# Hybrid SSD and pooling decoder step on one core: part-array stretches gathered, step sizes stored by group, and half products summed in PSUM

## The chip, the cores and the metric

The kernel runs on one core of a Trainium2 chip. The metric is the device time of one execution in microseconds (us): the median of three runs. Engines are named as in the profile: PE is TensorE's matmul, PEld its weight load, DVE is VectorE, ACT ScalarE, POOL GpSimd, SP SyncE, which issues most DMAs.

## The reference

One inference step of a trunk of two layers, an SSD (Mamba-2) layer and a causal pooling layer, each with adaLN modulation, RMSNorm, a gate and a residual, for a prompt of 1024 tokens and 8 samples of 8 new tokens, which the kernel lays side by side as 1088 columns. D_MODEL is 1024, D_INNER 2048; the scan has 8 groups of 4 heads (64 rows each), a state of 128 and chunks of 128 tokens, so 8 chunks in the prompt.

```python
zxbcdt = h @ w_in                                   # z, x, B, C, dt
xs, Bm, Cm = split(silu(conv4(xbc)))
dt = softplus(dt_raw + dt_bias); A = -exp(a_log)
acum = cumsum(dt * A, in the chunk)                 # cumulated decays
CB = einsum('bctgn,bcsgn->bctsg', C, B)
y_intra = (CB * exp(acum_t - acum_s) * mask) @ (x * dt)
chunk_states = einsum(B, exp(acum_end - acum), x * dt)
h_{c+1} = exp(acum_end) * h_c + chunk_states        # scan over chunks
y_inter = einsum(C, exp(acum), h_c)
out = rmsnorm_per_group((y_intra + y_inter + d_skip * x) * silu(z)) @ w_out
# pooling layer: uz = h @ w_in; windowed means of u; group matmul; * silu(z); @ w_out
```

## The kernel before, in words

**Products in three matmuls.** Every large product is made in fp32r from a high and a low half of both factors: three matmuls (hi*hi, hi*lo, lo*hi) into one PSUM bank (mm1, L179 to L184). ACT makes the high half, DVE or POOL the low one (split_half, L168 to L177).

**Front, about 100 to 360 us.** Twelve pairs of row blocks of the first projection (table FRONT, front_pairs L1412) and fourteen of the pooling layer's (fast_pairs L1036, about 1050 to 1340 us) go through fast_pair (L986): for the outputs u and z over two token halves of 544 columns, seven half products B11, B21, T2, T3, T1, T4, B22 in place of eight (Strassen's scheme in Winograd's form, with weight sums from w_sums L935 on POOL). A half product (product, L966) is 24 matmuls of 272 columns (L980 to L982) into two PSUM banks, about 3.0 us. DVE adds the results (add, L991) in SBUF; ACT makes one copy per pair (L1006). Between the pairs of kind b or x stands the causal convolution of the pair before (conv_tile L336): a chain of four steps per tile on DVE (L349) and then one Silu per tile on ACT (L352).

**Scan, about 364 to 930 us.** ssd_layer (L1458) drives scan_group (L504) for eight groups, and between its steps a second stream of full-array matmuls, the "fill" (beside: projections of later groups, then the output product). The table FILL (L51) says how many pieces of fill follow each step of a group. In a group, front(c) of a chunk makes B^T C and three transposes (L545, L549), the decays M on ACT (L556, L557) from acb, the cumulated decays of the group's 4 heads broadcast to 128 partitions by a DMA (load_ac L524), the scaled x, and Bt, B's transpose (L566). For two chunks at a time, states (L583) makes two S products (L588) and two updates of the state h: a POOL multiply (L596) and a DVE add (L597; for chunk 0 a copy, L593). Then rows (L601) makes y: matmuls M by x (L609) and h by C (L613), with 128x64 tiles, two of them side by side in the array. Part of the array is also used by the samples' transposes (L437), by Z (L628), the samples' y (L641, L644), adaLN's am (L253) and the sums of squares ms (L708). The program's scheduler orders each engine's instructions by priority; waits are by semaphores.

**Step sizes.** The cumulated decays ac are stored by one DMA as 128 partitions x 320; load_ac reads four rows of 512 B for each of 128 partitions.

## Time and profile before

| | |
|---|---|
| median of 3 runs | 1631.19 us (1631.13 to 1631.39) |
| profiled execution, its own time | 1633.98 us |
| span of the profiled execution, first to last instruction | 1632.2 us |
| mean granted TensorE clock | 0.994 |
| PE busy | 1601.1 us (98%), 12061 records |
| PEld busy | 1524.7 us (93%) |
| DVE, ACT, POOL busy | 1290.3 (79%), 816.7 (50%), 495.2 us (30%) |
| DMA | 275.60 MB, mean 169 GB/s |

PE's busy time is modelled, since matmuls overlap in the array: a row's duration is longer than the step to the next row. What a matmul costs is therefore read in the timeline as the distance from its start to the start of the next one. A timeline row "x4" holds four records in a run; a plain fp32 matmul leaves two records, one per pass, an fp32r matmul and a transpose leave one.

### The profile page before, as it was taken

How to read it: one execution, taken by the hardware profiler on the slowest of the kernel's cores; microseconds unless marked ns; L12 is line 12 of the kernel's file. 1: busy time of each engine (PE TensorE's matmuls, PEld its weight loads, DVE VectorE, ACT ScalarE, POOL GpSimd, SP SyncE). 2: the span in 40 equal slices, each digit the busy share in tenths (PEclk: the TensorE clock that was granted, in tenths of full speed). 3: DMA queues.
4: the chain of work that ended last, by engine and by line, in shares of the span. 5: the costliest groups of instructions: out<-in, count | busy, mean ns of one | idle time of the engine just before them, and what ended most of it. 6: DMA issues, size and time to landing. Idle time of an engine off the chain costs nothing.

```text
span 1632.2 us, 30956 instructions
## 1 busy us (share of the span) xinstructions
PE 1601.1 (98%) x12061; PEld 1524.7 (93%) x12061; DVE 1290.3 (79%) x2140; ACT 816.7 (50%) x1565; POOL 495.2 (30%) x527
## 2 busy tenths in 40 slices
PE   8999999999999999999999999999999999999997
PEld 6899999998899888988998899999999999999997
DVE  6875779777788888789887867988889867577876
ACT  6653334456776767575645536632322333333364
POOL 0233556511221202121212222366667640000241
PEclk9999999999999999999999999999999999999999
DMA  9422232264555554668898533043333369565783
GB/s 346 163 98 84 93 109 71 105 203 133 183 162 167 165 186 135 217 232 299 276 332 284 201 137 111 29 142 112 102 112 99 129 213 367 166 170 173 167 164 119
DMA packets 122306, 275.60 MB, mean 169 GB/s; under 512 B 18192, under 2 KB 59312, under 8 KB 122160
## 3 DMA queue, kind: packets, MB, share of 16 engines
q1 hardware_dynamic: 118128, 260.91, 46.8%
q0 software_dynamic: 4032, 12.72, 4.5%
q8 instruction: 95, 1.56, 0.4%
q14 instruction: 51, 0.42, 0.1%
HBM read 201.12 MB, written 70.23 MB: 166 GB/s over the span
## 4 chain that ended last, share of the span: by engine, by line
PE 82%; DVE 7%; DMA 5%; issue 3%; ACT 2%; POOL 1%; SPq 0%; DVEq 0%; ACTq 0%; POOLq 0%
PE st L982 11%; PE st L980 11%; PE st L981 11%; PE mm L182 10%; PE mm L184 10%; PE mm L183 10%; DMA acb<-acd 2%; PE op L1197 2%; PE op L1198 2%; PE op L1196 2%; PE y L609 2%; PE S L588 2%; PE y L613 2%; PE am L253 1%; PE tr L549 1%
## 5 line engine op out<-in xcount | busy, mean ns | idle before, releaser
L982 PE MATMUL st<-hh,w 128*128 128x272 f32 x832 | 240.8, 289 | 2.3 <-DVE w L176 2.3
L980 PE MATMUL st<-hh,w 128*128 128x272 f32 x832 | 240.2, 289 | 0.0
L981 PE MATMUL st<-hl,w 128*128 128x272 f32 x832 | 239.7, 288 | 0.0
L982 PE MATMUL st<-t,w 128*128 128x272 f32 x624 | 179.6, 288 | 0.0
L980 PE MATMUL st<-t,w 128*128 128x272 f32 x624 | 179.6, 288 | 0.0
L981 PE MATMUL st<-t,w 128*128 128x272 f32 x624 | 179.2, 287 | 0.0
L182 PE MATMUL mm<-hh,wh 128*128 128x364 f32 (+1 forms) x528 | 178.4, 338 | 0.1
L184 PE MATMUL mm<-hh,wl 128*128 128x364 f32 (+1 forms) x528 | 174.6, 331 | 0.0
L183 PE MATMUL mm<-hl,wh 128*128 128x364 f32 (+1 forms) x528 | 173.7, 329 | 0.0
L174 ACT ACTIVATE w<-wr 128x512 fp32r<-128x512 f32 x104 | 65.6, 631 | 190.4 <-PE st L982 156.8
L982 PEld LDWEIGHTS st<-hh,w 128*128 128x128 f32 x832 | 156.4, 188 | 3.4 <-DVE w L176 3.4
L980 PEld LDWEIGHTS st<-hh,w 128*128 128x128 f32 x832 | 156.7, 188 | 0.3 <-issue 0.3
L981 PEld LDWEIGHTS st<-hl,w 128*128 128x128 f32 x832 | 156.8, 188 | 0.0
L596 POOL TENSOR_TENSOR hd<-h,cd 128x256 f32<-128x256 f32 x56 | 47.1, 842 | 353.6 <-DVE h L597 195.4
L182 PE MATMUL mm<-gh,wh 128*128 128x364 f32 (+1 forms) x384 | 130.2, 340 | 2.1 <-ACT raw L419 2.1
L1197 PE MATMUL op<-b,w 128*128 128x272 f32 x448 | 129.0, 288 | 1.3 <-DVE b L1126 1.3
L1198 PE MATMUL op<-b,w 128*128 128x272 f32 x448 | 129.0, 288 | 0.7 <-DVE w L1170 0.7
L1196 PE MATMUL op<-b,w 128*128 128x272 f32 x448 | 129.6, 289 | 0.0
L184 PE MATMUL mm<-gh,wl 128*128 128x364 f32 (+1 forms) x384 | 127.1, 331 | 0.0
L183 PE MATMUL mm<-gl,wh 128*128 128x364 f32 (+1 forms) x384 | 126.7, 330 | 0.1
L980 PEld LDWEIGHTS st<-t,w 128*128 128x128 f32 x624 | 117.7, 189 | 0.0
L982 PEld LDWEIGHTS st<-t,w 128*128 128x128 f32 x624 | 117.3, 188 | 0.0
(293 smaller groups left out, 4613.7 us busy)
## 6 DMA issues: line engine op xcount, KB each, us to landing
wr<-win SPq DMA_DIRECT2D x48, 512.0 KB, 3.7
acb<-acd SPq DMA_DIRECT2D x64, 256.0 KB, 3.9
wr<-pin SPq DMA_DIRECT2D x32, 512.0 KB, 3.6
wr<-pout SPq DMA_DIRECT2D x28, 512.0 KB, 3.9
x<-x1d SPq DMA_DIRECT2D x24, 544.0 KB, 6.3
x1d<-x SPq DMA_DIRECT2D x22, 544.0 KB, 5.4
wr<-pout POOLq DMA_DIRECT2D x20, 512.0 KB, 5.5
x<-xT SPq DMA_DIRECT2D x16, 544.0 KB, 6.0
```

The lines of the kernel that those rows point to most:

```text
L174: self.nc.scalar.activation(hi, src, AF.Copy)
L182: nc.tensor.matmul(ps[:, :n], hi[:, k, :], ah[:, a:a + n], start=first, stop=False)
L183: nc.tensor.matmul(ps[:, :n], hi[:, k, :], al[:, a:a + n], start=False, stop=False)
L184: nc.tensor.matmul(ps[:, :n], lo[:, k, :], ah[:, a:a + n], start=False, stop=last)
L588: nc.tensor.matmul(S[:, 256 * i:256 * i + 256], Bt, xde.rearrange("p r q -> p (r q)"), start=True, stop=True)
L596: nc.gpsimd.tensor_tensor(out=hd, in0=h[-1], in1=cd.unsqueeze(2).to_broadcast([P, 4, 64]), op=ALU.mult)
L980: nc.tensor.matmul(ps[c][:, :QUART], hi[:, k], xh[:, t], start=(k == 0), stop=False)
L981: nc.tensor.matmul(ps[c][:, :QUART], hi[:, k], xl[:, t], start=False, stop=False)
L982: nc.tensor.matmul(ps[c][:, :QUART], lo[:, k], xh[:, t], start=False, stop=(k == 3))
L1196: nc.tensor.matmul(ps[:, :QUART], hi[:, k], xh, start=k == 0, stop=False)
L1197: nc.tensor.matmul(ps[:, :QUART], hi[:, k], xl, start=False, stop=False)
L1198: nc.tensor.matmul(ps[:, :QUART], lo[:, k], xh, start=False, stop=k == 7)
```

## The change

It has three parts.

**Part-array stretches gathered.** rows becomes visit: the matmuls of y for two chunks stand in one stretch of high priority, and the first of them waits for the second update of the state (`behind`), though their data need only the first. What else uses part of the array is placed right behind that stretch: adaLN's am behind the visits of chunks 0, 2 and 6 (ADA) and no longer among the projections, the samples' transposes and Z behind the one of chunk 4, the samples' y behind the one of chunk 6, ms of a group behind the first visit of the next one, and now in the PSUM bank S. FILL puts three pieces of fill ahead of a group's first step in groups 1 to 4.

On PE, in group 1, the first visit stood in two pieces with a matmul of the fill (mm) between them, and an S product in the first piece (y: output rows, M and xd: decays and scaled x, h: state, ea: scaled C):

```order
L609 MATMUL y_5143<-M_4979,xd_4988 64x128 x2
L609 MATMUL y_5144<-M_4979,xd_4988 64x128
L588 MATMUL S_5109<-xd_5076,Bt_5078 128x256
L609 MATMUL y_5144<-M_4979,xd_4988 64x128
L609 MATMUL y_5143<-M_5067,xd_5076 64x128 x2
L609 MATMUL y_5144<-M_5067,xd_5076 64x128 x2
L183 MATMUL mm_5159<-hl_668,wh_4835 128x360
L613 MATMUL y_5143<-ea_5060,h_5112 64x128 x2
L613 MATMUL y_5144<-ea_5060,h_5112 64x128 x2
L184 MATMUL mm_5159<-hh_667,wl_4836 128x360
```

In the changed kernel the same visit is one piece, followed by ms of group 0 and am:

```order
L185 MATMUL mm_5292<-hl_455,wh_4867 128x360
L622 MATMUL y_5062<-M_4990,xd_4999 64x128 x2
L622 MATMUL y_5063<-M_4990,xd_4999 64x128 x2
L622 MATMUL y_5062<-M_5012,xd_5021 64x128 x2
L629 MATMUL y_5062<-ea_5005,h_5031 64x128 x2
L622 MATMUL y_5063<-M_5012,xd_5021 64x128 x2
L629 MATMUL y_5063<-ea_5005,h_5031 64x128 x2
L752 MATMUL ms_5076<-z_4644,ones 32x272 x4
L256 MATMUL am_5081<-wr_4744,scp 32x256 x4
L256 MATMUL am_5081<-wr_4863,scp 32x256 x4
L555 MATMUL tr_5098<-xbc_4436,xbc_4179 128x128
```

So S and the fill no longer stand between the part-array matmuls.

At the second visit of group 1, PE had the matmuls that need no new state right behind S and the transposes, and 17 matmuls of fill (from the last row on) before those that need the first update:

```order
L588 MATMUL S_5263<-xd_5215,Bt_5217 128x256
L545 MATMUL tr_5278<-xbc_4520,xbc_4302 128x128
L549 MATMUL tr_5278<-kc,xbc_4796 128x128
L549 MATMUL tr_5278<-kc,xbc_4952 128x128
L549 MATMUL tr_5278<-kc,xbc_4302 128x128
L609 MATMUL y_5299<-M_5127,xd_5136 64x128 x2
L613 MATMUL y_5299<-ea_5120,h_5114 64x128 x2
L609 MATMUL y_5300<-M_5127,xd_5136 64x128 x2
L613 MATMUL y_5300<-ea_5120,h_5114 64x128 x2
L609 MATMUL y_5299<-M_5206,xd_5215 64x128 x2
L609 MATMUL y_5300<-M_5206,xd_5215 64x128 x2
L182 MATMUL mm_5319<-hh_393,wh_4997 128x364
```

Now there are four transposes and six matmuls of fill between the last S and the visit, whose first row waits for the second update:

```order
L596 MATMUL S_5164<-xd_5112,Bt_5114 128x256
L555 MATMUL tr_5183<-xbc_4436,xbc_4179 128x128
L557 MATMUL tr_5183<-kc,xbc_4675 128x128
L557 MATMUL tr_5183<-kc,xbc_4848 128x128
L557 MATMUL tr_5183<-kc,xbc_4179 128x128
L185 MATMUL mm_5292<-hl_617,wh_4867 128x360
L186 MATMUL mm_5292<-hh_616,wl_4868 128x360
L184 MATMUL mm_5292<-hh_668,wh_4867 128x360
L185 MATMUL mm_5292<-hl_669,wh_4867 128x360
L186 MATMUL mm_5292<-hh_668,wl_4868 128x360
L184 MATMUL mm_5292<-hh_707,wh_4867 128x360
L622 MATMUL y_5236<-M_5046,xd_5055 64x128 x2
```

The visit moved behind the fill, and all of it stands behind the wait.

**Step sizes by group.** They are stored as [chunk, head, token], by four DMAs and one for the samples, and load_ac reads one row of 2 KB for each partition.

**Half products in PSUM.** The order is B11, B21, T2, T1, T3, T4, B22. The banks X sum B11, T2, T3 and T4 one after the other, the banks Y sum T1 and B22. ACT keeps copies of X after B11, T2 and T3 (keep), so that the sums that end elsewhere can be formed by DVE; z's first half goes from X through ACT straight to its place, with its Silu.

On ACT, in a pair that follows one of kind b or x, before: the copy of the first product (u<-st), weight splits (w), the convolution's two Silus (xbc), a gate's Silu (z):

```order
L1006 ACTIVATE u_2345<-st_2350 128x272
L1006 ACTIVATE u_2345<-st_2351 128x272
L174 ACTIVATE w_2379<-sw_2216 128x512
L174 ACTIVATE w_2411<-wr_2181 128x512
L352 ACTIVATE xbc_2316<-xbc_2316 128x1088
L352 ACTIVATE xbc_2329<-xbc_2329 128x1088
L862 ACTIVATE z_2343<-z_2343 128x544
```

And now (u_2051 is the first copy, u_2052 the one after T2, then u_2051 again after T3):

```order
L1052 ACTIVATE u_2051<-st_2053 128x272
L1052 ACTIVATE u_2051<-st_2054 128x272
L176 ACTIVATE w_2088<-wr_1894 128x512
L176 ACTIVATE w_2117<-wr_1894 128x512
L359 ACTIVATE xbc_2019<-xbc_2019 128x1088
L359 ACTIVATE xbc_2032<-xbc_2032 128x1088
L1052 ACTIVATE u_2052<-st_2053 128x272
L1052 ACTIVATE u_2052<-st_2054 128x272
L176 ACTIVATE w_2150<-sw_1925 128x512
L176 ACTIVATE w_2182<-wr_1923 128x512
L1052 ACTIVATE u_2051<-st_2053 128x272
L1052 ACTIVATE u_2051<-st_2054 128x272
```

The copy after T2, on which T3's matmuls into the same banks wait, stands behind the two Silus.

The diff, cut to its core:

```diff
-FILL = (((1,) * 10 + (2,),) * 4 + ((1,) * 9 + (4, 5),) + ((3, 2, 2, 2, 2, 2, 2, 2, 2, 2, 3),) * 2 + ((2, 2, 2, 1, 1, 1, 1, 1, 2, 2, 1),))
+FILL = ((1,) * 10 + (2,),) + (((3, 0, 0) + (1,) * 7 + (2,),) * 3 + ((3, 0, 0) + (1,) * 6 + (4, 5),) + ((3, 2, 2, 2, 2, 2, 2, 2, 2, 2, 3),) * 2 + ((2, 2, 2, 1, 1, 1, 1, 1, 2, 2, 1),))
+ADA = (0, 2, 6)
+HIGH = 400
...
+        self.last_mm = nc.tensor.matmul(ps[:, :n], lo[:, k, :], ah[:, a:a + n], start=False, stop=last)
...
+    def behind(self, ins, other):
+        self.tc.add_manual_dep(ins.ins, other.ins.name, mybir.DependencyInfo(mybir.DependencyClass.Sync, mybir.DependencyReason.DATA), reason="behind")
...
-        nc.sync.dma_start(self.acd, ac)
+        for j in range(4):
+            nc.sync.dma_start(self.acd[2 * j:2 * j + 2].rearrange("c h t -> h c t"), ac[32 * j:32 * j + 32, :256].rearrange("h (c t) -> h c t", c=2))
+        nc.sync.dma_start(self.acs, ac[96:128, 256:320])
...
+                src = self.acd[c, 4 * g:4 * g + 4]
...
+            nc.sync.dma_start(t.rearrange("p r t -> p (r t)"), src.rearrange("r t -> (r t)").unsqueeze(0).to_broadcast([P, t.shape[1] * t.shape[2]]))
...
+        def visit(c, F, F8=None, zsc=None):
 
             py = [pp.tile([P, 512], F32, tag="y", bufs=2, name=self.name("y")) for _ in range(2)]
-            for i in range(2):
-                tok, M, xdt, _, _, _, ct = F[i]
-                hc, a = h[-3 + i], 128 * i
-                for q in range(2):
-                    for rr in range(2):
-                        r, o = 2 * q + rr, slice(64 * rr, 64 * rr + 64)
-                        nc.tensor.matmul(py[q][o, a:a + 128], xdt[:, r, :], M[:, r, :], start=True, stop=(hc is None))
-                    if hc is not None:
+            py8 = None
+            with self.tc.high_priority(HIGH):
+                mm = None
+                for i in range(2):
+                    tok, M, xdt, _, _, _, ct = F[i]
+                    hc, a = h[-3 + i], 128 * i
+                    for q in range(2):
                         for rr in range(2):
                             r, o = 2 * q + rr, slice(64 * rr, 64 * rr + 64)
-                            nc.tensor.matmul(py[q][o, a:a + 128], hc[:, r, :], ct[:, r, :], start=False, stop=True)
+                            m = nc.tensor.matmul(py[q][o, a:a + 128], xdt[:, r, :], M[:, r, :], start=True, stop=(hc is None))
+                            if mm is None:
+                                mm = m
+                                self.behind(mm, hins[-1])
+                        if hc is not None:
+                            for rr in range(2):
+                                r, o = 2 * q + rr, slice(64 * rr, 64 * rr + 64)
+                                m = nc.tensor.matmul(py[q][o, a:a + 128], hc[:, r, :], ct[:, r, :], start=False, stop=True)
...
+                with self.tc.issue_after(m.ins):
+                    if c == 0:
+                        next(rest, None)
+                    if c == 4:
+                        self.pts = pp.tile([P, 512], F32, tag="tr", bufs=2, name=self.name("tr"))
+                        for i, t in enumerate((xs[0], xs[1], B)):
+                            self.dup(self.pts[:, 128 * i:128 * i + 128], t[:, NP:TOK])
+                        nc.tensor.matmul(self.pts[:64, 384:448], B[:, NP:TOK], C[:, NP:TOK], start=True, stop=True)
+                        Z = sample_products()
...
+                    if (g, c) in self.ada_plan:
+                        self.ada = self.ada_do(self.ada_plan[g, c])
+                        next(self.ada)
...
+        ps = self.pp.tile([P, 512], F32, tag="S", bufs=1, name=self.name("ms"))
...
+            yield self.split_half(s[:, f])
+            nc.gpsimd.tensor_tensor(out=s[:, l], in0=u[:, l], in1=s[:, l], op=ALU.subtract)
             yield self.split_half(z[:, f])
...
+                nc.tensor.matmul(ps[c], hi[:, k], xh[:, t], start=first and k == 0, stop=False, skip_group_check=True)
+                nc.tensor.matmul(ps[c], hi[:, k], xl[:, t], start=False, stop=False, skip_group_check=True)
+                nc.tensor.matmul(ps[c], lo[:, k], xh[:, t], start=False, stop=k == 3, skip_group_check=True)
...
+        s, s2 = (self.tp.tile([P, HALF], F32, tag="mt2", bufs=self.nmt2, name=self.name("u2")) for _ in range(2))
+        def keep(t, x):
+            for c in range(2):
+                nc.scalar.activation(t[:, cs[c]], x[c], AF.Copy)
...
+        X = self.banks("mm")
+        product(X, "B11")
+        keep(s, X)
...
+        after("B11")
+        V = self.banks("tr")
+        product(V, "B21")
         for c in range(2):
-            nc.scalar.activation(s[:, cs[c]], ps[c], AF.Copy)
-        after("B11")
-        ps = product(("tr", "tr"), "B21")
+            put(u, 0, c, V[c], s[:, cs[c]])
+        after("B21")
+        product(X, "T2", False)
+        keep(s2, X)
+        after("T2")
+        Y = self.banks("y")
+        product(Y, "T1")
+        after("T1")
+        product(X, "T3", False)
+        keep(s, X)
         for c in range(2):
-            put(u, 0, c, ps[c], s[:, cs[c]])
-        after("B21")
-        ps = product(("y", "y"), "T2")
+            put(z, 1, c, Y[c], s[:, cs[c]])
+            after(f"z1{c}")
+        after("T3")
+        product(X, "T4", False)
         for c in range(2):
-            add(s[:, cs[c]], ps[c], s[:, cs[c]])
-        after("T2")
-        ps = product(("mm", "S"), "T3")
+            o = z[1] + QUART * c
+            nc.scalar.activation(z[0][:, o:o + QUART], X[c], AF.Silu if gate else AF.Identity)
+        after("T4")
+        product(Y, "B22", False)
         for c in range(2):
-            add(z1[:, cs[c]], ps[c], s[:, cs[c]])
-        after("T3")
-        ps = product(("mm", "mm"), "T1")
-        for c in range(2):
-            add(s[:, cs[c]], ps[c], s[:, cs[c]])
-            put(z, 1, c, ps[c], z1[:, cs[c]])
-            after(f"z1{c}")
-        after("T1")
-        ps = product(("tr", "tr"), "T4")
-        for c in range(2):
-            put(z, 0, c, ps[c], z1[:, cs[c]])
-            after(f"z0{c}")
-        after("T4")
-        ps = product(("y", "y"), "B22")
-        for c in range(2):
-            put(u, 1, c, ps[c], s[:, cs[c]])
+            put(u, 1, c, Y[c], s2[:, cs[c]])
...
-            sc = self.scan_group(g, T[g])
+            sc = self.scan_group(g, T[g], rest)
             for i, n in enumerate(FILL[g]):
-                next(sc)
+                if i or not g:
+                    next(sc)
                 for j in range(n):
                     next(self.fill)
-                    if i in (0, 3) and j == 0:
+                    if i in (0, 3, 5) and j == 0:
                         next(rest, None)
+                if g and not i:
+                    with self.tc.issue_after(self.last_mm.ins):
+                        next(sc)
```

More of the change, by code (lines that the diff above doesn't have):

```diff
@@ L411, in proj_group @@
                 self.proj_evict(G, ii, raw, ps, c)
-                if c:
-                    next(ada, None)
                 yield
@@ L675, in scan_group @@
             states(c, F)
-            if c == 6:
-                load_z()
-            Fn = [front(c + 2)]
-            if c == 6:
-                self.slots.free(B)
-            rows(c, F)
-            F = Fn
-            if c == 6:
-                zsc = sample_inter()
-                self.slots.free(C)
+            next(self.ada, None)
+            if c < 6:
+                Fn = [front(c + 2)]
+            if c == 2:
+                load_h0()
+                sample_prep()
+            elif c == 6:
+                load_z()
             yield
             if c < 6:
-                F.append(front(c + 3))
+                zsc = visit(c, F)
+                Fn.append(front(c + 3))
+                F = Fn
                 if c == 4:
-                    load_h0()
+                    F8 = front(8)
+                    self.slots.free(B, C)
+            else:
+                py = visit(c, F, F8, zsc)
+            if c < 6:
                 yield
-        F, h = F[0], h[-1]
+        next(self.ada, None)
+        h = h[-1]
         nc.sync.dma_start(self.io["hpT"][g], h.rearrange("p r q -> p (r q)"))
-        st = back_sample(F, zsc)
+        st = back_sample(F8, py)
         yield
@@ L979, in product, with banks, fast_pair @@
             for k, (xh, xl) in enumerate(self.X[x]):
[L980 to L985 removed]
+                nc.tensor.matmul(ps[c], hi[:, k], xh[:, t], start=first and k == 0, stop=False, skip_group_check=True)
+                nc.tensor.matmul(ps[c], hi[:, k], xl[:, t], start=False, stop=False, skip_group_check=True)
+                nc.tensor.matmul(ps[c], lo[:, k], xh[:, t], start=False, stop=k == 3, skip_group_check=True)
+    def banks(self, tag):
+        return [self.pp.tile([P, 512], F32, tag=tag, bufs={"mm": 3, "tr": 2, "y": 2}[tag], name=self.name("st"))[:, :QUART] for _ in range(2)]
+    def fast_pair(self, u, z, after, gate):
         nc, product = self.nc, self.product
[L990 to L991 removed]
         def put(dst, half, c, x, y):
@@ L1479, in ssd_layer @@
         self.out_unit()
-        next(rest)
+        for _ in range(3):
+            next(rest)
         for _ in range(2):
```

111 lines of the change are left out of this document (51 added, 60 removed).

## The prediction

> **What bounds the kernel now.** First the page's busy times, then the windows by stage (columns: window, PE, PEld, DVE, ACT, POOL busy with counts, granted clock, DMA share, GB/s), then PE's waits.
>
> ```profile
> PE 1601.1 (98%) x12061; PEld 1524.7 (93%) x12061; DVE 1290.3 (79%) x2140; ACT 816.7 (50%) x1565; POOL 495.2 (30%) x527
> ```
>
> ```profile
> 400.00:450.00 50.00, 50.00 (x384) 44.47 (x383) 39.09 (x63) 33.11 (x71) 9.36 (x19) 1.00 0.52 169
> 900.00:950.00 50.00, 46.30 (x357) 41.98 (x356) 39.74 (x78) 23.97 (x55) 9.73 (x10) 0.97 0.57 197
> 1200.00:1250.00 50.00, 50.00 (x401) 50.00 (x400) 43.90 (x64) 15.61 (x28) 31.78 (x23) 1.00 0.35 112
> ```
>
> ```profile
> PE S L588 <- ACT Bt L566: 4.5, 3, 2.3
> PE st L982 <- DVE w L176: 2.3, 5, 0.6
> ```
>
> PE is the bound in every stage. In the pairs of 1200 to 1250 us it has no gap, so DVE work that disappears there is worth nothing. What can still be won is inside PE's own "busy" time (matmuls that start later than their work asks), and in a few waits of some 15 us in all. So two questions decide: what PE loses between neighbouring matmuls, and which waits the new orders add.
>
> **Term 1: changes between full and part array.** One visit of the scan in PE's timeline (start, duration, then the instruction):
>
> ```profile
> 454.30 0.49 PE L549 MATMUL tr<-kc,xbc 128*128 128x128 f32 x3
> 454.72 0.44 PE L609 MATMUL y<-M,xd 128*64 128x128 f32 x4
> 454.99 0.39 PE L613 MATMUL y<-ea,h 128*64 128x128 f32 x4
> 455.21 0.39 PE L609 MATMUL y<-M,xd 128*64 128x128 f32 x4
> ...
> 455.65 0.61 PE L609 MATMUL y<-M,xd 128*64 128x128 f32 x8
> 456.19 0.43 PE L182 MATMUL mm<-hh,wh 128*128 128x364 f32 x1
> 456.46 0.33 PE L183 MATMUL mm<-hl,wh 128*128 128x364 f32 x1
> 456.62 0.33 PE L184 MATMUL mm<-hh,wl 128*128 128x364 f32 x1
> ```
>
> Four y records in the middle take 0.22 us from start to start (454.99 to 455.21), so 0.11 per pass of two side by side; a full matmul takes 0.16 to 0.17. Against these: the three transposes before the stretch take 0.42 in place of 0.33 (+0.09), the first four y 0.27 (+0.05), the last eight 0.54 in place of 0.44 (+0.10), and the first full matmul behind 0.27 (+0.10). One excursion from full to part and back costs 0.34 us beyond its work. Where the fill cuts a visit, the matmul in between pays too:
>
> ```profile
> 446.45 0.43 PE L183 MATMUL mm<-hl,wh 128*128 128x360 f32 x1
> 446.82 0.66 PE L613 MATMUL y<-ea,h 128*64 128x128 f32 x8
> 447.41 0.43 PE L184 MATMUL mm<-hh,wl 128*128 128x360 f32 x1
> ```
>
> That one takes 0.37 from start to start (446.45 to 446.82). Between two kinds of part-array tiles there is a price as well:
>
> ```profile
> 489.55 0.33 PE L641 MATMUL y<-M,xd 64*64 64x64 f32 x4
> 489.81 0.34 PE L644 MATMUL y<-kc,zsc 128*64 128x64 f32 x4
> 490.08 0.33 PE L641 MATMUL y<-M,xd 64*64 64x64 f32 x4
> ```
>
> Half the columns of the rows above should take 0.11; they take 0.26, so such a change costs about 0.15. In the two programs' PE order I count the changes: excursions from full to part fall from 99 to 51, changes between kinds of part tiles rise from 33 to 58, since am, ms, Z and the samples' y now follow a visit directly. 48 x 0.34 = 16.3 less 25 x 0.15 = 3.75: **-12.6 us**. PE stands without gaps there (400 to 450 us), so all of it counts. Bounds: 0 if the price turns out to be hidden elsewhere, -16.3 if inner changes are free.
>
> The Trainium skill, page "TensorEngine Tiling (Array Packing)", section Tiling Modes, says that a change of the tiling mode, not of the tile, drains TensorE; it gives no figure. By that rule a change to another part mode costs like one to the full array, so 25 x 0.17 in place of 25 x 0.15, which moves the sum by half a microsecond, and placing ms and am (32-column tiles) behind y (64-column ones) saves less than "gathered" suggests; the rows at 489.55 agree.
>
> **Term 2: the visit's new wait.** The first y matmul now waits for the second update of h. Queued behind it on PE is the whole visit and all fill. The chain at its best and at its worst, from PE, DVE and POOL rows:
>
> ```profile
> 480.36 1.13 PE L588 MATMUL S<-xd,Bt 128*128 128x256 f32 x4
> 481.42 0.27 PE L545 MATMUL tr<-xbc,xbc 128*64 128x64 f32 x1
> ```
>
> ```profile
> 481.60 0.42 DVE L597 TENSOR_TENSOR h<-hd,S 128x256 f32<-128x256 f32 x1 [0.70 <-PE S L588]
> 482.75 0.42 DVE L597 TENSOR_TENSOR h<-hd,S 128x256 f32<-128x256 f32 x1 [0.73 <-POOL hd L596]
> ```
>
> ```profile
> 457.07 1.36 DVE L358 SCALAR_TENSOR_TENSOR raw<-raw,cwh,raw 128x1112 f32<-128x1112 f32 x1
> 458.36 0.41 DVE L597 TENSOR_TENSOR h<-hd,S 128x256 f32<-128x256 f32 x1
> ```
>
> At best the second update ends at 483.17, 1.75 us after PE's next instruction behind S started (481.42). In the changed order I add up what PE has between S and the visit. At the second visit of seven groups that is four transposes (454.30 row: 0.33 for three, and 0.22 for the two-pass one) and six full matmuls of 0.166: 1.55 us, so 0.2 to 0.3 short, 7 x 0.25 = 1.8 us. The first visits have 2.2 to 2.5 us, the third and fourth 1.8 to 5.7: enough at best. But DVE is 80% busy there and works in order; the row at 458.36 shows an update right behind a convolution step of 1.36 us. The changed order has the scaling by the row norms (L720), which stood ahead of it here too, behind the update; a convolution step can still run when S lands. For half of one such step in two visits in fourteen with short cover I add 1.2: **+3 us**. Bounds: 0, and 14 x 1.35 = 19.
>
> ms in the S bank adds a wait of the second visit's S for ACT's logarithm:
>
> ```profile
> L301 ACT ACT_TABLE_LOAD x11 | 14.1, 1283 | 8.2 <-PE ms L708 8.1
> L711 ACT ACTIVATE z<-ms,eps 128x272 f32<-128x272 f32 x8 | 3.9, 488 | 0.1
> ```
>
> Load, am's step and logarithm take about 2.2 us; am, transposes, eight full matmuls and am's end stand between ms and S on PE, about 3.0. Covered, 0; if ACT comes a microsecond late, 4 x 0.3.
>
> **Term 3: T3 behind the copy.** The fifth product now adds into the banks that ACT copies after T2, and in ACT's order that copy stands behind the convolution's Silus. The pair that starts at 204.61 on PE, with ACT and DVE:
>
> ```profile
> 216.66 0.29 PE L980 MATMUL st<-hh,w 128*128 128x272 f32 x1
> 216.79 0.29 PE L981 MATMUL st<-hl,w 128*128 128x272 f32 x1
> 217.52 0.40 PE L982 MATMUL st<-hh,w 128*128 128x272 f32 x1 [0.45 <-DVE w L176]
> ```
>
> ```profile
> 206.03 10.83 DVE L349 SCALAR_TENSOR_TENSOR xbc<-raw,vec,xbc 128x1024 f32<-128x1024 f32 x8
> 216.78 0.69 DVE L176 TENSOR_TENSOR w<-sw,w 128x512 fp32r<-128x512 f32 x1
> ```
>
> ```profile
> 207.49 0.75 ACT L1006 ACTIVATE u<-st 128x272 f32<-128x272 f32 x2
> 215.70 2.31 ACT L352 ACTIVATE xbc<-xbc 128x1088 f32<-128x1088 f32 x2 [4.14 <-DVE xbc L349]
> ```
>
> The fifth product starts at 216.66; the Silus, fed by DVE's chain, end at 218.01, a copy takes 0.38 (0.75 for two), so T3 can start at 218.4: 1.75 us late. The old wait at this place, for the low half of the weights (0.73 for a step of 0.125, so 0.6), disappears under it. Five pairs have it (the waits row: five times): 5 x (1.75 - 0.6) = **+5.7 us**. Bounds: -3 if the copy is in time, +11 if both Silus start only when the chain ends (216.8 + 2.3 + 0.4). The other copies have a product of 3.0 us, or half of one, between them and the next use of the bank: 0. The 208 adds less on DVE and 104 copies more on ACT lie beside a saturated PE: 0.
>
> **Term 4: cumulated decays.**
>
> ```profile
> 902.23 0.21 ACT L574 ACTIVATE cd<-acb 128x4 f32<-128x4 f32 x1 [1.56 <-DMA acb<-acd]
> ```
>
> ```profile
> 903.21 0.70 PE L588 MATMUL S<-xd,Bt 128*128 128x256 f32 x2 [2.35 <-ACT Bt L566]
> ```
>
> 64 loads of one row of 2 KB instead of four of 512 B shorten such waits. PE waits here once, 2.35 us, mostly since the load was issued late: **-1 us**; bounds 0 and -10 (the scan's PE waits and the slow matmuls behind them). Four more stores on SP, once, during the front: 0.
>
> **Sum.** 1633.98 - 12.6 + 5.7 + 3 - 1 = 1629.1 for an execution like the profiled one. That one lies 2.8 us above the median (1631.19), so **1626.3** in its terms.
>
> **Rivals.** *Updates late at the visits, slower than before.* Everything behind the first y of 32 visits waits with it. Without term 2 the change gains 7.9; from 0.25 us per visit nothing is left, and from 0.35 it is slower. If DVE has a convolution step ahead of the update in the 14 visits with short cover, 14 x 1.35 = 19 replaces the 3: 1642; if in half of them, 1633. For it: the row at 458.36. Against: at the best rows DVE waits for S, and the scaling is moved.
>
> *T3 isn't late.* Then the five waits are simply gone, 5 x 1.75 less: 1617.5. For it: fewer adds on DVE. Against: the chain of 10.83 us starts as soon as the pair before ends, and no add lies within it.
>
> *The scan's long waits vanish* with shorter loads and the other order of the scan: another 7 us, 1619. For it: the 4.5 us of S on Bt, with the load behind them. Against: issue time, not transfer, is late at 902.
>
> *The gathering doesn't pay*, since inner changes cost like excursions and waits hide the rest: term 1 at -4, 1635.
>
> *The waits at T3 halve the clock.* After the wait of 2.35 us at 903.21 these rows follow:
>
> ```profile
> 904.99 0.64 PE L613 MATMUL y<-ea,h 128*64 128x128 f32 x4
> 905.42 0.64 PE L609 MATMUL y<-M,xd 128*64 128x128 f32 x4
> ```
>
> Four y take 0.43 us where the rows at 454.99 have 0.22: half speed. If five waits of 1.75 us did the same for 3.5 us of matmuls each, 5 x 1.75 more: 1635. Against: the five waits of 0.6 of today are followed by steps of 0.125 as before.
>
> The Trainium skill, page "TensorE: Matmul & The Clock Gate", Part 1, has the clock halved only after an idle window of about 3.4 us, so by it a wait of 1.75 us would be free of this. The rows at 904.99 show half speed after a shorter wait than that, so here the measurement decides, and the case keeps a chance.
>
> **How the numbers follow.** A measurement tells 0.2% (3.3 us): faster is below 1627.9, slower above 1634.5. Forecast, 1622 to 1631: 0.43, of which 0.28 lie below 1627.9. T3 in time: 0.14, scan waits gone: 0.17, both faster. Late updates: 0.16 (0.11 slower). The gathering not paying, or clock losses at T3: 0.05 each (0.07 slower). Faster 0.59, slower 0.18, same 0.23. The range goes from 1615, which takes in a rival's gain, to 1637, halfway into the late updates.
>
> **What would show it.** For term 2, PE's waits must list y behind DVE's h, seven times at 0.2 to 0.3 us. For term 3, the half products' first matmul must wait for ACT's copy five times, about 1.7 us each. In the scan, the first full matmul after a part stretch (0.27) should appear about 50 times rather than 100. The acb loads should land in under 3.9 us. Wrong would make it above all an update of h that DVE does later than S plus 2 us in most groups.

## The result and the profile after

The changed kernel takes 1655.67 us (median of 4 runs, 1653.44 to 1657.81) against 1631.29 before (4 runs): **ratio 1.0146, 95% interval 1.0128 to 1.0163, slower by 24 us**. The forecast was 1626.3, with a range that ended at 1637. The profiled execution took 1656.07, its span 1654.3 us.

The page's busy times, and the windows and PE waits that answer to those of before:

```profile
PE 1598.1 (97%) x12061; PEld 1529.5 (92%) x12061; DVE 1230.2 (74%) x1932; ACT 849.5 (51%) x1700; POOL 512.1 (31%) x527
```

```profile
400.00:450.00 50.00, 47.71 (x357) 44.67 (x356) 39.37 (x55) 31.86 (x68) 10.98 (x15) 0.97 0.42 127
900.00:950.00 50.00, 45.30 (x353) 41.45 (x352) 39.10 (x80) 26.32 (x71) 10.16 (x9) 1.00 0.76 261
1200.00:1250.00 50.00, 50.00 (x401) 50.00 (x401) 36.67 (x45) 18.84 (x39) 29.16 (x21) 1.00 0.34 111
```

```profile
PE y L622 <- DVE h L605: 15.3, 17, 2.7
PE st L1025 <- ACT u L1052: 8.4, 6, 1.7
PE S L596 <- ACT Bt L574: 8.3, 5, 2.3
```

DVE lost 60 us of work and PE has exactly as many matmuls as before; the pooling pairs (1200 to 1250) are full on PE either way. What changed is that PE waits in the scan: 400 to 450 had no gap before. Where the 22.1 us between the two spans lie, from the starts of PE's rows (first and last half product of each series, last ms of the scan):

| stage | before | after |
|---|---|---|
| up to the first half product | 96.2 | 96.4 |
| front pairs | 258.6 | 262.8 |
| scan, to the last ms | 587.5 | 605.5 |
| between scan and pooling pairs | 115.4 | 115.3 |
| pooling pairs | 294.9 | 296.9 |
| from there to the end | 279.5 | 277.3 |

The scan carries 18 of them. I split its PE time into three: changes of tile mode at the prediction's prices (0.34 us for an excursion from full to part, 0.15 between part tiles), long waits (steps from one matmul's start to the next of over 0.48 us, less 0.2 for the matmul), and the rest. The last column is not a fourth part: it says for how long the granted clock was half in the scan, by the trace's record of the clock.

| scan, us | excursions, inner changes | their price | long waits | rest | clock at half |
|---|---|---|---|---|---|
| before | 82, 33 | 32.8 | 8.6 | 546.1 | 6.8 |
| after | 34, 58 | 20.3 | 31.3 | 553.9 | 17.1 |

So the number of mode changes fell as forecast. Their price falls by 12.5 us, but that is the count times the prediction's prices, not a measured saving. The long waits rose by 22.7 us, most of it at y (PE's waits for h) and some 4 at S. The rest rose by 7.8: a stretch at half clock loses at most half its length, so up to 5.1 of it is the clock (8.5 against 3.4), the remainder short waits and what the split doesn't name.

The dearest waits sit at the fourth visit (chunk 6) of groups 1 to 4. The one in group 1, on PE, DVE and POOL:

```profile
496.45 0.33 PE L186 MATMUL mm<-hh,wl 128*128 128x364 f32 x1
498.74 0.44 PE L622 MATMUL y<-M,xd 128*64 128x128 f32 x4 [1.95 <-DVE h L605]
```

```profile
491.38 0.28 DVE L567 TENSOR_TENSOR cb<-tr,kc 128x128 f32<-128x128 f32 x1
491.58 0.68 DVE L570 TENSOR_TENSOR xd<-tr,tkx 128x512 f32<-128x512 f32 x1
492.17 1.62 DVE L568 TENSOR_TENSOR M<-M,cb 128x512 f32<-128x512 f32 x1
493.72 2.43 DVE L583 TENSOR_TENSOR ea<-xbc,ea 128x512 f32<-128x512 f32 x1
...
497.13 0.40 DVE L605 TENSOR_TENSOR h<-hd,S 128x256 f32<-128x256 f32 x1
```

```profile
491.31 4.29 POOL L685 TENSOR_TENSOR h<-h,ea 128x1024 f32<-128x1024 f32 x2
497.62 0.61 POOL L604 TENSOR_TENSOR hd<-h,cd 128x256 f32<-128x256 f32 x1 [2.02 <-DVE h L605]
```

PE's last matmul ahead of the visit starts at 496.45, the visit waits 1.95 us for the second update of h. DVE has two operations of 128x512 ahead of the first update that take 1.62 and 2.43 us. Both stretch while POOL runs L685, the decay of the samples' states, two steps of 1.94 and 2.39 us. The second of them ends at 496.15, 0.55 us behind POOL's last step (495.60), as if it had been held until then. All 13 operations of these two lines (L568, L583) that overlap L685 in this trace take 1.0 to 2.4 us; elsewhere they take 0.7, and 1.1 in five of the cases beside POOL's multiply L604. The operations beside L685 that read one input from PSUM (L567 and L570 read tr) keep their 0.28 and 0.68. POOL itself isn't what the update waits for: it is idle for 2.02 us ahead of its part of the second update (L604).

In the kernel before, POOL ran the same two steps (L647) only behind the fourth visit, and one of the two DVE operations stretched there as well. But no PE work waited for what DVE did then. PE, DVE and POOL before:

```profile
484.08 1.07 PE L628 MATMUL Z<-h,ctm 128*32 128x256 f32 x16
```

```profile
486.03 1.98 DVE L575 TENSOR_TENSOR ea<-xbc,ea 128x512 f32<-128x512 f32 x1
```

```profile
485.29 4.52 POOL L647 TENSOR_TENSOR h<-h,ea 128x1024 f32<-128x1024 f32 x2 [0.26 <-issue]
```

By the times, what held the decay back there was Z, which reads the samples' states that the decay overwrites. In all eight groups the decay starts 0.5 to 1.9 us behind the start of the last Z matmul (0.51 or 0.52 in six), although its other input, ea of the samples, had been there since 473.04 in group 1. The change put Z behind the visit of chunk 4, one visit earlier, and that freed the states. Only ea, which ends at 490.89, and two short copies of POOL's then stood ahead of the decay, and it passed ahead of the fourth visit's update. PE and ACT after:

```profile
486.97 1.07 PE L670 MATMUL Z<-h,ctm 128*32 128x256 f32 x16
```

```profile
490.49 0.40 ACT L552 ACTIVATE ea<-acb 128x256 f32<-128x256 f32 x1
```

The Trainium skill, page "GPSIMD Engine Reference", section Specifications, says that POOL's SBUF interfaces are shared with VectorE and that DVE instructions with two SBUF inputs contend. The trace agrees, and gives the size: 0.68 becomes 1.62 and 2.43 us.

The waits cost more than their length. In group 2, behind the same wait, from PE's timeline:

```profile
575.61 0.44 PE L622 MATMUL y<-M,xd 128*64 128x128 f32 x4 [1.95 <-DVE h L605]
575.88 0.39 PE L629 MATMUL y<-ea,h 128*64 128x128 f32 x4
576.10 0.39 PE L622 MATMUL y<-M,xd 128*64 128x128 f32 x4
...
577.11 0.64 PE L629 MATMUL y<-ea,h 128*64 128x128 f32 x4
577.54 0.64 PE L622 MATMUL y<-M,xd 128*64 128x128 f32 x4
```

The four records take 0.22 us at first and 0.43 some 1.5 us later. The Trainium skill, page "TensorE: Matmul & The Clock Gate", Part 1, halves the clock after an idle window of about 3.4 us; here half speed follows a wait of 1.95 us, so the measurement decides against it as a bound.

Behind the equally long wait of group 1 the clock stays full. The two windows (the third figure from the end is the granted clock):

```profile
498.80:501.80 3.00, 3.00 (x52) 2.56 (x56) 2.50 (x5) 2.02 (x4) 1.40 (x4) 1.00 0.32 75
576.50:579.50 3.00, 3.00 (x30) 2.43 (x29) 1.53 (x4) 0.99 (x2) 0.45 (x3) 0.50 0.39 118
```

The trace's record of the clock shows the difference. Leaving out the first 100 us and the program's end, half clock starts at 415.94, 576.37, 654.88, 733.38 and 1047.41 us, and lasts 3.41 us each time (6.83 at 654.88). These starts lie 47, 23, 23 and 92 steps of 3.413 us apart, so they stand on a fixed grid. The fourth visits' waits of groups 2 to 4 each have at least 1.95 us of idle time within the one step of that grid just before the clock falls. The wait of group 1 (496.79 to 498.74) is cut in two by a grid point at 497.86. In the run with the copy ahead of the Silus (below) it is the other way round: group 1's wait lies within one step and half clock follows at 498.73, group 2's is cut and none follows. So which of these waits is followed by half speed depends on where the grid falls in that execution. No sharp bound for the idle time comes out: in the run with POOL's decay later a step with 1.23 us of it was followed by half clock (725.1) and one with 1.90 us was not (752.4).

In the front, the pair of before's 216.66, now on ACT and PE:

```profile
216.50 2.31 ACT L359 ACTIVATE xbc<-xbc 128x1088 f32<-128x1088 f32 x2 [4.00 <-DVE xbc L356]
218.72 0.38 ACT L1052 ACTIVATE u<-st 128x272 f32<-128x272 f32 x1
```

```profile
217.53 0.28 PE L1027 MATMUL st<-hh,w 128*128 128x272 f32 x1
219.15 0.39 PE L1025 MATMUL st<-t,w 128*128 128x272 f32 x1 [1.33 <-ACT u L1052]
```

T3 starts right behind the copy, and the copy stands behind the two Silus: the third term of the prediction, as told. T3 comes 1.62 us behind the matmul before it, 1.49 more than a step of 0.125.

### The profile page after: what moved, and what is told of

It is laid out like the page before. It is cut to its first block, busy times and chain, and to the rows that moved or that the text cites. A ratio compares the mean times of both kernels' runs of the same rounds, so it can differ in the third digit from the quotient of the medians.

```text
span 1654.3 us, 30633 instructions
## 1 busy us (share of the span) xinstructions
PE 1598.1 (97%) x12061; PEld 1529.5 (92%) x12061; DVE 1230.2 (74%) x1932; ACT 849.5 (51%) x1700; POOL 512.1 (31%) x527
## 5 line engine op out<-in xcount | busy, mean ns | idle before, releaser
L604 POOL TENSOR_TENSOR hd<-h,cd 128x256 f32<-128x256 f32 x56 | 52.0, 928 | 275.0 <-DVE h L605 125.3
L1052 ACT ACTIVATE u<-st 128x272 f32<-128x272 f32 x156 | 60.5, 395 | 114.3 <-PE st L1027 112.5
```

Source lines behind the costliest of these rows:

```text
L604: nc.gpsimd.tensor_tensor(out=hd, in0=h[-1], in1=cd.unsqueeze(2).to_broadcast([P, 4, 64]), op=ALU.mult)
L1052: nc.scalar.activation(t[:, cs[c]], x[c], AF.Copy)
```

## The experiments

Each run is set against runs of the kernel before on the same chip.

**POOL's decay later.** In the changed kernel, the two steps of L685 wait for the second update of h:

```diff
-                nc.gpsimd.tensor_tensor(out=h0[i], in0=h0[i],
+                d = nc.gpsimd.tensor_tensor(out=h0[i], in0=h0[i],
...
+                self.behind(d, hins[-1])
```

> The changed kernel, with POOL's decay of the samples' states (L685, two of 2.15 us a group) held behind the second update of h of a group's fourth visit, where it stood before the change. Theory P (POOL: this decay was pulled ahead of the update and holds up DVE's operations with two SBUF inputs, L568 and L583, which stand ahead of the update): the four waits of the fourth visits (2.0, 2.0, 2.0, 2.8) go, the half-speed stretches behind three of them (about 6.6) too, and the waits at 405 to 419 in group 0 (about 4): 1637 to 1641. Theory V (each visit pays for the second update whatever POOL does): at most 3 us less, 1653 to 1656.

1640.29 us (before 1631.39; ratio 1.0049, 1.0033 to 1.0065): 15.4 less than the change's 1655.67. The same place in its trace, DVE and POOL:

```profile
488.90 0.68 DVE L568 TENSOR_TENSOR M<-M,cb 128x512 f32<-128x512 f32 x1
489.50 0.68 DVE L583 TENSOR_TENSOR ea<-xbc,ea 128x512 f32<-128x512 f32 x1
```

```profile
492.92 4.81 POOL L685 TENSOR_TENSOR h<-h,ea 128x1024 f32<-128x1024 f32 x2 [0.59 <-issue]
```

The two operations are back at 0.68, POOL's steps come after them, and the scan is 590.8 us long instead of 605.5. PE's waits for h at the visits fall from 15.3 to 7.1 us, those of S for Bt from 8.3 to 5.5, and the clock is at half for 6.8 us of the scan in place of 17.1. The pair of POOL steps that moved ahead in each group accounts for nearly two thirds of the loss of 24.

**Only the data's waits.** In the changed kernel:

```diff
-                                self.behind(mm, hins[-1])
+                                pass
```

> The changed kernel without the extra wait of a visit's first matmul for the second update of h; only the data's own waits are left, and the scheduler cuts the visits in pieces again, with am, ms, Z gathered as before. Theory P: the update is late all the same; the waits shrink by at most 1.1 us each, and some 40 excursions of 0.34 come back: 1650 to 1665. Theory V: most of the 15.3 us of waits for h go, 1640 to 1648.

1668.06 (ratio 1.0231, 1.0211 to 1.025): slower still. Visits are cut up again: 110 excursions and 57 inner changes in the scan, 46.0 us at the prediction's prices, against 20.3 in the changed kernel and 32.8 before. The long waits fall from 31.3 to 16.8 us and the rest stays (553.0). PE now waits for the y banks to be read out:

```profile
PE y L622 <- DVE xbc L588: 10.1, 5, 2.9
```

So the bare wait isn't the cause by itself; without it the scheduler finds another order, and that one is worse.

**Copy ahead of the Silus.** In the changed kernel the Silus are held behind the copy after T2:

```diff
+        k2 = keep(s2, X)
+        for i in self.silus:
+            self.behind(i, k2)
```

> The changed kernel, with the two Silus of the convolution (L359) held on ACT behind the copy after T2. If the copy behind the Silus is what T3 waits for, the 8.4 us of waits for ACT's copies in the front go: 1647. If the wait only moves (to the next sums, or to the Silu's readers), 1652 to 1656.

1655.6 (ratio 1.0146): nothing. The wait only moved:

```profile
PE st L1025 <- ACT u L1052: 6.9, 6, 2.6
```

The second of the two copies after T2 now stood behind a gate's Silu that waits for DVE, whose sums stand behind the convolution's chain, and the copy after T3 stood behind the Silus.

**All copies free.** The same with the Silus and that gate's Silu held behind the copy after T3.

```diff
         product(X, "T3", False)
-        keep(s, X)
+        k3 = keep(s, X)
+        for i in self.silus:
+            self.behind(i, k3)
...
+                    if x == "B21":
+                        self.silus.append(i)
```

> The changed kernel, with what stood in the way of the copies held on ACT behind the copy after T3: the convolution's two Silus and the gate's Silu of the first half (the one that the second copy was stuck behind in the run before). If the front's waits come only from ACT's order, the 8.4 us go but for five waits of 0.45 for the low half of the weights: 1648 to 1650. If DVE's chain is the real limit (the copy after T3 needs a buffer that DVE's late sum still reads), waits of over a microsecond stay: 1653 to 1656.

1651.49 (ratio 1.0124, 1.0105 to 1.0143): 4.2 less. The front takes 258.9 us, as before the change, and the waits for ACT's copies there are gone; what is left there is the wait for the low half of the weights:

```profile
PE st L1027 <- DVE w L178: 2.8, 5, 1.0
```

It was 2.3 us in five waits before the change, and was hidden under the wait for the copies in the changed kernel. T3's wait was therefore worth 4.2 us net, not 8.4.

**One part at a time.** First the half products as before the change, with the two other parts kept (w_sums, product, fast_pair and their callers taken back):

```diff
-        product(X, "T2", False)
-        keep(s2, X)
+        ps = product(("y", "y"), "T2")
+        for c in range(2):
+            add(s[:, cs[c]], ps[c], s[:, cs[c]])
```

> The changed kernel with the seven half products as before the change (order, sums by DVE, weight sums), the two other parts kept. The front is then 4.2 us shorter, as measured between the two traces, and the pooling pairs 1 to 2 us: 1650 to 1652. If the half products cost more than the front shows (order of later stages), less than 1648.

1647.23 (ratio 1.0101, 1.0076 to 1.0125), 8.4 less than the change.

Then the half products alone, on the kernel before (the same functions taken over):

```diff
-        ps = product(("y", "y"), "T2")
+        product(X, "T2", False)
+        keep(s2, X)
```

> The kernel before, with only the seven half products summed in PSUM. By the front's and the pooling pairs' difference in the traces: 1631.3 + 4.2 + 2 = 1637. By the run that undid this part: 1631.3 + 8.4 = 1640. If DVE's 208 sums less give something back in other stages, 1632 to 1635.

1637.4 (before 1631.09; ratio 1.0035, 1.0023 to 1.0047): the half products cost 6.3 us by themselves, 4.2 of it in the front (258.6 to 262.8), 1.2 in the pooling pairs. DVE's 208 sums less give nothing back.

And the step sizes alone, on the kernel before:

```diff
-        nc.sync.dma_start(self.acd, ac)
+        for j in range(4):
+            nc.sync.dma_start(self.acd[2 * j:2 * j + 2].rearrange("c h t -> h c t"), ac[32 * j:32 * j + 32, :256].rearrange("h (c t) -> h c t", c=2))
...
+                src = self.acd[c, 4 * g:4 * g + 4]
```

> The kernel before, with only the step sizes stored by group and read as one row of 2 KB. Forecast -1 us by the prediction's term; if the waits for these loads are about their issue, 0: 1630 to 1632. If shorter loads bring the scan's waits forward, down to 1625.

1629.4 (ratio 0.9998, 0.9983 to 1.0013): no difference that can be told. In the changed kernel's trace the loads land no sooner either (median 4.5 us, 3.9 before).

**Visits without the half products.** Parts one and two with POOL's decay held, half products as before: two of the edits above together.

```diff
+                self.behind(d, hins[-1])
...
-        product(X, "T2", False)
+        ps = product(("y", "y"), "T2")
```

> Parts one and two of the change (visits, step sizes) with the half products as before, and POOL's decay held behind the update. By the sum of the two runs before (15.4 us less for the decay, 8.4 less for the products): 1631 to 1633. If the gathering pays once POOL is out of the way, as the count of 12.6 us has it, under 1625; if each return from a plain fp32 matmul to an fp32r one costs like one from a part of the array (0.08 us, more of them than before), 1629 to 1634.

1633.87 (ratio 1.0013, 0.9997 to 1.003). The two causes add up to within 2 us (1655.7 - 15.4 - 8.4 = 1631.9), and the gathering still shows no gain.

**Both mends, then the looser wait.** The changed kernel with POOL's decay and the Silus held:

```diff
+                self.behind(d, hins[-1])
...
+            self.behind(i, k3)
```

> The changed kernel with both mends: POOL's decay held behind the second update, and the Silus held behind the copy after T3. If the two causes are independent, 1655.7 - 15.4 - 4.2 = 1636. If they share time (the scan's start depends on the front's Silus), 1638 to 1641.

1637.33 (before 1629.68; ratio 1.0047, 1.0032 to 1.0062). Then also, for the visit's first matmul, the first update in place of the second:

```diff
-                                self.behind(mm, hins[-1])
+                                self.behind(mm, hins[-2])
```

> As the run with both mends, and the visit's first matmul waits for the first update of h in place of the second, which is all that its data need; the visit stays in one piece. Theory: the waits for h left over (7.1 us in 13 visits with POOL out of the way) are the price of the stricter wait; the first update is 1.1 us earlier, so 4 to 6 us less: 1630 to 1632. Rival: the visit then stands ahead of fill that covered the wait before, since the order shifts with it, and nothing is won: 1635 to 1637.

1631.58 (ratio 1.0012, 1.0 to 1.0023): 5.7 less. PE's waits for h in the visits, first with the second update:

```profile
PE y L622 <- DVE h L605: 4.8, 12, 1.0
```

and with the first one, where only one wait of a sample's y is left:

```profile
PE y L645 <- DVE h L605: 1.6, 1, 1.6
```

The stricter wait, which the data don't ask for, cost 5.7 us. The scan by the split above, for the three steps:

| scan, us | length | price of mode changes | long waits | rest | clock at half |
|---|---|---|---|---|---|
| POOL's decay later | 590.8 | 20.3 | 19.1 | 551.4 | 6.8 |
| both mends | 587.9 | 20.3 | 19.8 | 547.8 | 0 |
| wait for the first update | 582.0 | 21.6 | 12.9 | 547.5 | 0 |

Here the scan is shorter than before the change (587.5): 11.2 from mode changes at their price, less 4.3 of waits and 1.4 of rest. But part of these 5.5 us is the clock. The profiled execution took 1628.28 us, the fastest of its ten, and its scan has no stretch at half clock; the one profiled before took 1633.98 and has 6.8 us of it, which is up to 3.4 us of time. With that taken off, the scan is only some 2 us shorter and the rest is about 5 longer.

**Low half on POOL.** The kernel before with the step sizes by group, and the changed kernel with all mends, both with POOL making one more low half:

```diff
-POOLW = (3, 5)
+POOLW = (3, 4, 5)
```

> The kernel before with the step sizes stored by group, and the low half of the fifth split on POOL in place of DVE (POOLW 3, 4, 5). The five waits of the fifth product for DVE (3.2 us with their slower first matmul) go, since POOL isn't behind the convolution: 1626 to 1628. If POOL's 1.9 us per split come too late in the pooling pairs, where POOL is at two thirds, 1630 or more.

1631.62 (ratio 1.0011, 1.0 to 1.0021). The gain that was expected didn't come: the front is 1.0 us shorter and the pooling pairs are 0.7 longer, and PE waits for POOL's late halves in their turn (2.1 us in two waits).

> The changed kernel with all mends: POOL's decay held, Silus held, wait for the first update, low half of the fifth split on POOL. From the run that waits for the first update, less 2.2 to 3.9 us for the five waits of T3 for DVE's low half: 1627 to 1630. If nothing was won by the first update, 1632 to 1634.

1636.98 (ratio 1.0043, 1.0028 to 1.0058): five microseconds worse than without it, and also not what was expected. The front falls to 256.3, but the pooling pairs grow from 296.6 to 306.5, since PE waits for POOL's late halves:

```profile
PE st L1028 <- POOL w L178: 7.7, 9, 1.5
```

**Mended, without the half products.** POOL's decay held, wait for the first update, half products as before.

```diff
+                self.behind(d, hins[-1])
...
-                                self.behind(mm, hins[-1])
+                                self.behind(mm, hins[-2])
...
-        product(X, "T2", False)
+        ps = product(("y", "y"), "T2")
```

> Parts one and two of the change with POOL's decay held and the wait for the first update, and the half products as before the change: what the runs so far point to as the fastest. From the run with all three parts (1631.6) less 0.3 us in the front and 1.7 in the pooling pairs: 1629 to 1630. If gathering is worth 12.6 us once no wait is in its way, 1618 to 1620; if its worth is what the traces leave (about 5 us), 1625 to 1630.

1630.51 (12 runs; before 1631.22; ratio 1.0002, 0.9987 to 1.0016). A gathering worth its 12.6 us would have given 1618 to 1620. By the split, this scan takes 585.4 us, 2.1 less than before the change: 11.2 less for mode changes, 5.5 more of long waits, 3.6 more of rest, and the rest's increase is about 5 when the clock is taken off (3.4 us at half here, 6.8 before). No version beat the kernel before by more than its measurement tells.

**What a return costs.** Behind each full fp32r matmul that follows a plain fp32 one in the full array, the next one starts 0.08 us late, and the traces hold more such places after the change (109 in the scan against 56). If that is a price, part of the excursion's 0.34 isn't saved by gathering. Probes on the run that waits for the first update, with work in every half product that nobody reads:

```diff
+                if c and k == 2:
+                    nc.tensor.transpose(pr[:, :128], self.ident, self.ident)
```

> A probe on the run that waits for the first update (1631.6): in each of the 182 half products one plain fp32 transpose of 128 columns more (into a spare PSUM bank that nobody reads), in the middle of the fp32r matmuls. Its own step is 0.109 us, 20 in all. If the first fp32r matmul behind a plain fp32 one in the full array pays 0.084 us, 182 x 0.193 = 35: 1666 to 1668. If only a change of tile size costs, 1651 to 1652.

```diff
+                    nc.tensor.transpose(pr[:, 128:256], self.ident, self.ident)
```

> The same probe with two transposes side by side in place of one. Own steps 182 x 0.218 = 39.7, and one return as before: 182 x 0.302 = 55, 1686 to 1688 with the cost of the return, 1671 without. The difference to the probe with one must be 182 x 0.109 = 20 either way, which checks the step.

```diff
-                    nc.tensor.transpose(pr[:, :128], self.ident, self.ident)
+                    for rr in range(2):
+                        nc.tensor.matmul(pr[64 * rr:64 * rr + 64, :128], self.ident[:, 64 * rr:64 * rr + 64], self.ident, start=True, stop=True)
```

> The same probe with a pair of 128x64 matmuls side by side (two passes, own step 0.218) in place of the transpose. With 0.34 us for the excursion of the tile mode: 182 x 0.56 = 102, 1733 to 1735. If part and full array differ in nothing but the return that a transpose pays too: 182 x 0.302 = 55, 1687.

One execution each: 1650.59, 1672.84 and 1727.57. Against 1631.58 that is 0.104, 0.227 and 0.527 us per half product. The kernel they start from varied from 1628.28 to 1638.40, so these are good to some 0.03; the spans of the front and the pooling pairs alone, where all half products lie, give 0.09, 0.18 and 0.52. PE's rows with one transpose, and with one pair of part-array matmuls:

```profile
1203.28 0.29 PE L1031 MATMUL st<-t,w 128*128 128x272 f32 x1
1203.40 0.27 PE L1028 MATMUL pr<-kc 128*128 128x128 f32 x1
1203.43 0.37 PE L1029 MATMUL st<-t,w 128*128 128x272 f32 x1
1203.64 0.29 PE L1030 MATMUL st<-t,w 128*128 128x272 f32 x1
1203.76 0.29 PE L1031 MATMUL st<-t,w 128*128 128x272 f32 x1
```

```profile
1202.51 0.29 PE L1032 MATMUL st<-hh,w 128*128 128x272 f32 x1
1202.73 0.44 PE L1029 MATMUL pr<-kc 128*64 128x128 f32 x4
1203.10 0.39 PE L1030 MATMUL st<-hh,w 128*128 128x272 f32 x1
1203.33 0.29 PE L1031 MATMUL st<-hl,w 128*128 128x272 f32 x1
1203.46 0.29 PE L1032 MATMUL st<-hh,w 128*128 128x272 f32 x1
```

With the transpose, 0.48 us from 1203.28 to 1203.76 less three steps of 0.125 leave 0.11: its own step, and nothing for the return. The 0.21 behind it is only where the rows start: the transpose's own row has 0.03. So the theory of a price for the return falls. With the part pair, 0.95 less 0.375 leaves 0.575, and less its own 0.22, 0.36 for the excursion; by the times 0.527 less 0.22, 0.31, and by the spans 0.30. The price of 0.34 lies between them.

## Why the prediction was wrong, point by point

**Term 1, mode changes: right in mechanism, its worth not shown.** The counts fell as forecast, and the price holds in a probe by itself (0.30 to 0.36) and in the run with only the data's waits, where 76 excursions more leave the rest nearly as it was. But -12.5 is the count times the price. In the run without the half products, with POOL's decay held and the looser wait, the scan is 2.1 us shorter and the time the same: waits take back 5.5 of the 11.2, and at equal clock some 5 more lie in the rest. What they are, no run shows. The rival "the gathering doesn't pay" (term 1 at -4) came nearer to this than the forecast.

**Term 2, the visit's wait: the step that failed.** The prediction had +3 us, from "a convolution step can still run when S lands", with bounds of 0 and 19. Long waits rose by 22.7, and the rest by 7.8, of which up to 5.1 is the clock behind such waits. The step compared the chain of updates on DVE and POOL at its best and at its worst, read from the order before, with the work between S and the visit. It looked for what else DVE had ahead of the update and called the third and fourth visits covered ("enough at best"). It didn't ask what the moved steps set free on POOL: with Z behind the visit of chunk 4, the decay L685 passes ahead of the fourth visit's update, and there it stretches two DVE operations from 0.68 to 1.62 and 2.43 us. That cost 15.4. The stricter wait itself cost 5.7, about twice the 3 forecast. The rival "updates late at the visits" named the right place; its worst time (1642) still fell short, since it had another cause, a convolution step ahead of the update.

**Term 3, T3 behind the copy: right, a little large.** +5.7 forecast, +4.2 measured in the front: T3 came 1.49 us late, not 1.75. Missed was the last pooling pair, where a copy stands on ACT behind work of the next stage (PE waits 1.75 us there); the pooling pairs grew by 2.0.

**Term 4, step sizes:** -1 forecast, no difference measured.

The case that waits of 1.75 us at T3 halve the clock didn't come: the front's steps behind them (waits of 1.33 us) are 0.125. Behind the fourth visits' waits of 2 us it did, in three of four groups of the profiled execution.

What stays open: with both mends and the looser wait, 4.3 us of long waits remain over before, spread over the samples' y, the fill and the transposes (S's waits for Bt, 4.7 us, are about as long as the 4.5 before), and the rest is some 5 us longer at equal clock without a named cause. The median shows none of the 5.5 us that the profiled scan gained; up to 3.4 of them are the clock, as told above.

## What to carry to other kernels

When a change moves a step earlier, list every instruction that becomes ready with it, on every engine, also those that only waited to overwrite what the step reads, and see what each stands ahead of. An engine that is idle two thirds of the time (POOL) can delay the one that matters, here by stretching DVE's operations from 0.68 to 2.43 us. A wait set stricter than the data need has a price at each place, to be read as the distance between the two events (here 1.1 us, 5.7 in sum). A count of events times a price is not yet a saving: here 11 to 12 us by count showed as none in the time. And when two profiled executions are compared, look first at how long each ran at half clock (6.8 us and none in the scan, above).

## What the runs showed of the hardware

- A DVE operation of 128x512 with two SBUF inputs took 1.62 and 2.43 us in place of 0.68 beside POOL's 128x1024 steps of 1.94 and 2.39 us; those with an input in PSUM kept their time.
- In the trace of the change PE's clock fell to half for 3.41 or 6.83 us, on a grid of 3.413 us. Waits of about 1.95 us were followed by it where they lay within one step of the grid, and not where a grid point cut them (group 1 after the change, group 2 in the run with the copy ahead of the Silus).
- A plain fp32 transpose between fp32r matmuls of the full array costs 0.09 to 0.11 us and no return; an excursion to a part of the array costs 0.30 to 0.36 us.
